# A hybrid decoder layer: group norms beside the latents, roots spread later, FFN matmul runs of 9, 9, 6

## The chip, the cores and the metric

The kernel runs on one core of one Trainium2 chip. The core has five engines that work side by side, each in the order of its own queue: TensorE (PE, with its weight loads as PEld), VectorE (DVE), ScalarE (ACT), GpSimd (POOL) and SyncE (SP, which issues transfers). They wait for each other by semaphores. The time is the device time of one execution in microseconds (us); what is compared is the median of several runs.

## The reference, cut to what matters

One layer with 256 tokens and a width of 2048, in float32. RMS norm, one input projection, two groups of heads side by side (16 RWKV-7 heads of 64 and 8 latent-attention heads), one output projection, residual; then RMS norm, a gated MLP of width 5632 with a causal convolution of width 3 on its gate, residual, and a final RMS norm.

```
h = rms_norm(x, attn_norm_g)
proj = h @ w_in
h_r, h_k, h_v, h_w, h_a, h_g = split(token_shift(proj[..., :RWKV_SHIFT_DIM], mu))
c_q, c_kv, k_pe = split(proj[..., RWKV_SHIFT_DIM:])          # 512, 512, 64 columns

# RWKV-7 group: a recurrence over the tokens, then a norm over each head
y = rwkv7_scan(r, decay, k, v, -kk, kk * a)
y = ((y - mean(y)) * rsqrt(var(y) + GN_EPS)) * gn_w + gn_b   # group norm
y_rwkv = (y + sum(r * k * r_k) * v) * (sigmoid(h_g) @ g2)

# latent attention group
q  = rms_norm(c_q, q_norm_g) @ w_uq
kv = rms_norm(c_kv, kv_norm_g) @ w_ukv
y_mla = softmax(causal(q @ k.T * scale)) @ v

x = x + concat(y_rwkv, y_mla) @ w_out
h = rms_norm(x, ffn_norm_g)
x = x + (silu(conv(h @ w_gate)) * (h @ w_up)) @ w_down
return rms_norm(x, final_norm_g)
```

## The kernel before

**Products.** Each float32 operand is split into a high part (hi, rounded to a matmul type) and the rest (lo), and a product is the sum of hi by hi, hi by lo and lo by hi. Weights come in pieces of 128x1024: `piece` lets SP load one, ACT cast it to hi and DVE subtract to get lo. `prod_c` multiplies a piece with 256 tokens at a time, `prod_a` with tokens on the output's partitions, and `prod_b`, used for the gate and up weights of the MLP, with moving blocks of 512 columns (256 of the activation's hi, 256 of its lo): 8 wide matmuls for the weight's hi, then 8 of 256 columns for its lo. `joined` and `scaled` take sums out of PSUM.

**Order.** The kernel's code emits operations; a scheduler simulates them and lays each engine's queue out by the place of emission as priority and by the buffers that it has (three PSUM buffers for sums called mm, three called ch, two called at). In the compiled program each engine's order is fixed. `tc.issue_after(x)` keeps an operation behind x, and `pend`/`flush` hand small jobs to the next tile.

**Stages.** (1) Input projection, tile by tile (`in_tile`), with the key, receptance and value tiles prepared for the recurrence. An opening part computes the decay: `wa` goes through a tanh on ACT and is multiplied by `lora`. (2) The recurrence: four chunks of 64 tokens (`chunk(c)`), serial, each with many small matmuls and copies between PE, DVE and ACT. The scheduler places tiles of the latents' projection between them. (3) `latent(0)` and `latent(1)`: four input tiles each for the query and the key-value latent, scaled out of PSUM into `cr`, split into `cl`, their squares summed in `css`; a sum over partitions (`pss`, copied to `ssm`), a root on POOL (`rsqrt`), the root `rr`, and by `bcast` (two matmuls with the diagonals `dg`, into `rsb`) its copy in all rows, `rrB`. (4) Up-projections: `up_b` for queries (`wuq`) and keys (`wuk`), `prod_a` for values (`wuv`). (5) `group_norm(w)` for each half w of the tokens: bonus values `bv`, means `gmu`, variances `gva` from squares `gsq`, a root of 16 columns on DVE, the norm's weights `gnw`, `gnb`, the gate `pgate` (two matmuls on `g2a`, `g2b`), then four transposes (`pyT`) and the split into `yhi`, `ylo` for the output projection. It is emitted behind all up-projections, interleaved with the attention heads (`heads`, with `scores` and `attend`). (6) Output projection, (7) MLP in two blocks of 24 and 20 tiles of 128 columns, (8) down-projection and final norm.

Of the kernel before, what the change touches and what calls it, by code (L numbers as in the profile page):

```python
# [54 lines left out]
def hybrid_layer(ctx: ExitStack, tc: tile.TileContext, a: dict, out: bass.AP):  # L55
# [109 lines left out]
    def prod_b(acc, pieces, act, kt0, n, first, last):  # L165
        hi, lo = pieces
        for j in range(n):
            PE.matmul(acc, hi[:, j * P:(j + 1) * P], act(kt0 + j), start=first and j == 0, stop=False,  # L168
                      skip_group_check=True)
        for j in range(n):  # L170
            PE.matmul(acc[:, :T], lo[:, j * P:(j + 1) * P], act(kt0 + j)[:, 0, :], start=False,  # L171
                      stop=last and j == n - 1, skip_group_check=True)

    def prod_c(acc, pieces, act, kt0, n, first, last):
        hi, lo = pieces
        for j in range(n):
            for s in range(2):
                PE.matmul(acc[:, :T], hi[:, j * P:(j + 1) * P], act(kt0 + j)[:, s, :],  # L178
                          start=first and j == 0 and s == 0, stop=False)
        for j in range(n):  # L180
            PE.matmul(acc[:, :T], lo[:, j * P:(j + 1) * P], act(kt0 + j)[:, 0, :], start=False,  # L181
                      stop=last and j == n - 1)
# [10 lines left out]
    def prod_a(accs, pieces, act_hi, act_lo, kt0, n, first, last, tbs=(0, 1)):  # L193
        hi, lo = pieces
        for j in range(n):
            wh, wl = hi[:, j * 512:(j + 1) * 512], lo[:, j * 512:(j + 1) * 512]
            for tb in tbs:
# [4 lines left out]
                PE.matmul(accs[tb], al, wh, start=False, stop=last and j == n - 1)  # L202
# [124 lines left out]
    S.activation(warm, ones[:, 0:2], AF.Sin)  # L327
# [78 lines left out]
    S.activation(wa[0:64], wa[0:64], AF.Tanh)
# [390 lines left out]
    def latent(x, gname, post):  # L797
# [22 lines left out]
        rb = con([P, T], f"rrB{x}")  # L820
        bcast(rr, rb, at, t2)
# [1 line left out]
        rrB.append(rb)
# [3 lines left out]
    latent(1, "kvg", 1.0)
    flush(True)
# [7 lines left out]

    def up_b(src, i, x, dsts):
        pcs = piece(src[i])
        for j in range(2):
            acc = mm()  # L840
            prod_c(acc, (pcs[0][:, j * 512:(j + 1) * 512], pcs[1][:, j * 512:(j + 1) * 512]),
                   lambda k: cl[x][k // 2][:, k % 2, :, :], 0, 4, True, True)
            scaled(dsts[j], acc, rrB[x])
# [8 lines left out]
    g2a = s4(n="g2a")  # L852
    g2b = s4(n="g2b")
    gnwb = [s4(n=n) for n in ("gnw", "gnb")]
    with tc.issue_after(ylast[1]):
        for t, n in zip(gnwb, ("gnw", "gnb")):
            nc.scalar.dma_start(t, a[n].broadcast_to([P, 1024]))
        nc.scalar.dma_start(g2a, a["g2"][0:P])
# [134 lines left out]
    for blk, nf in enumerate((24, 20)):  # L993
        hh = [s4(F32R, "hh").rearrange("p (k t) -> p k t", k=4) for _ in range(nf // 4)]
        hl = [s4(F32R, "hl").rearrange("p (k t) -> p k t", k=4) for _ in range(nf // 4)]
        for fi in range(nf):
# [1 line left out]
            accs = []
            for gu in range(2):
                acc = mm()  # L1000
                for h in range(2):
                    prod_b(acc, piece(a["wgu"][f, gu, h]), z_hl, h * 8, 8, h == 0, h == 1)
                accs.append(acc)
# [126 lines left out]
```

## Time and profile before

| | |
|---|---|
| median of 3 runs | 1191.4 us (1191.02 to 1200.56) |
| profiled execution | 1189.71 us |
| its span | 1187.9 us |
| mean granted TensorE clock | 0.993 |
| PE busy | 1161.1 us (98%), 7673 matmuls |
| DVE busy | 807.2 us (68%) |
| ACT busy | 590.5 us (50%) |
| POOL busy | 32.7 us (3%) |
| read from HBM | 210.58 MB, 180 GB/s over the span |

The span is the time between the first and the last record of the profiled execution. Rows of the timeline begin with the start in us from the span's beginning and the duration in us; then come the engine, the line, the operation, output and inputs, the shapes and the number of operations that the row groups. Brackets give idle time of that engine ahead of the row and what ended it.

### The profile page before, as it was taken

Reading aid. Unit: us, or ns where it says so; the run is one execution under the profiler, and the core shown is the slowest. Engines: PE = TensorE matmul, PEld = TensorE weight load, DVE = VectorE, ACT = ScalarE, POOL = GpSimd, SP = SyncE. Lnnn points to the kernel's source line nnn. Section 1 sums busy time; section 2 is a strip of 40 time slices with the busy share of each in tenths; the row PEclk is TensorE's granted clock in tenths of the full one; section 3 lists DMA queues with packets and bytes.
Section 4 is the critical chain, followed back from the end, with each engine's and each line's share of the span. In section 5 each row is a group of like instructions: output and inputs, shape, how many; then the busy total and the mean of one; then the engine's idle time right before and its main releaser. Section 6 shows DMA issues by size and latency. Waiting matters only on the chain.

```text
span 1187.9 us, 19414 instructions
## 1 busy us (share of the span) xinstructions
PE 1161.1 (98%) x7673; PEld 1022.6 (86%) x7673; DVE 807.2 (68%) x1301; ACT 590.5 (50%) x895; POOL 32.7 (3%) x87
## 2 busy tenths in 40 slices
PE   8999999998979999999999999999999999999996
PEld 8899999987958888888888888888888888888885
DVE  5898669745976567777777775444577777775663
ACT  6794345433425456555555554333455555544541
POOL 1200000003000001000000000000000000000000
PEclk9999999998999999999999999999999999999998
DMA  8635455714425555555555555665555555566662
GB/s 312 219 113 178 134 171 194 228 43 152 155 89 178 165 188 178 196 194 188 187 193 194 189 188 192 192 197 189 201 189 191 189 195 194 186 226 210 198 217 82
DMA packets 71035, 215.98 MB, mean 182 GB/s; under 512 B 17616, under 2 KB 17872, under 8 KB 70944
## 3 DMA queue, kind: packets, MB, share of 16 engines
q1 hardware_dynamic: 69776, 211.84, 54.3%
q10 hardware_dynamic: 768, 2.05, 0.5%
q0 software_dynamic: 400, 0.85, 0.3%
q8 instruction: 60, 0.98, 0.3%
q14 instruction: 31, 0.25, 0.1%
HBM read 210.58 MB, written 3.41 MB: 180 GB/s over the span
## 4 chain that ended last, share of the span: by engine, by line
PE 90%; DVE 4%; DMA 2%; POOL 1%; ACT 1%; issue 1%; SPq 0%; ACTq 0%; DVEq 0%; POOLq 0%
PE mm L168 27%; PE mm L171 14%; PE mm L178 10%; PE mm L200 9%; PE mm L201 9%; PE mm L202 9%; PE mm L181 5%; PE pg L545 1%; DVE lo L139 1%; PE px L694 1%; PE py L694 1%; DMA xraw<-in_xT 1%; DMA xt<-in_x 1%; DVE bv L752 0%; DMA raw<-in_win 0%
## 5 line engine op out<-in xcount | busy, mean ns | idle before, releaser
L139 DVE TENSOR_TENSOR lo<-raw,hi 128x1024 fp32r<-128x1024 f32 x376 | 459.9, 1223 | 278.7 <-ACT hi L138 273.5
L138 ACT CAST hi<-raw 128x1024 fp32r<-128x1024 f32 x376 | 395.0, 1051 | 471.8 <-PE mm L202 126.3
L168 PE MATMUL mm<-z,hi 128*128 128x512 f32 x1408 | 351.2, 392 | 0.0
L168 PEld LDWEIGHTS mm<-z,hi 128*128 128x128 f32 x1408 | 251.9, 188 | 43.7
L171 PEld LDWEIGHTS mm<-z,lo 128*128 128x128 f32 x1408 | 188.2, 188 | 14.5
L171 PE MATMUL mm<-z,lo 128*128 128x256 f32 x1408 | 191.5, 278 | 0.0
L178 PE MATMUL mm<-x,hi 128*128 128x256 f32 x1024 | 137.9, 283 | 2.1 <-ACT x L148 1.4
L178 PEld LDWEIGHTS mm<-x,hi 128*128 128x128 f32 x1024 | 126.0, 190 | 5.8 <-issue 1.7
L201 PE MATMUL mm<-lo,hh 128*128 128x512 f32 x336 | 130.7, 389 | 0.0
L202 PE MATMUL mm<-hi,hl 128*128 128x512 f32 x336 | 130.7, 389 | 0.0
L200 PE MATMUL mm<-hi,hh 128*128 128x512 f32 x336 | 119.7, 389 | 0.0
L202 PEld LDWEIGHTS mm<-hi,hl 128*128 128x128 f32 x336 | 63.1, 188 | 13.1
L200 PEld LDWEIGHTS mm<-hi,hh 128*128 128x128 f32 x336 | 63.1, 188 | 13.1
L201 PEld LDWEIGHTS mm<-lo,hh 128*128 128x128 f32 x336 | 63.1, 188 | 13.0
L181 PE MATMUL mm<-x,lo 128*128 128x256 f32 x512 | 73.7, 281 | 0.1
L181 PEld LDWEIGHTS mm<-x,lo 128*128 128x128 f32 x512 | 65.0, 188 | 1.1 <-issue 0.7
L201 PE MATMUL mm<-lo,yhi 128*128 128x512 f32 x128 | 51.1, 399 | 0.0
L202 PE MATMUL mm<-hi,ylo 128*128 128x512 f32 x128 | 50.3, 394 | 0.0
L200 PE MATMUL mm<-hi,yhi 128*128 128x512 f32 x128 | 49.5, 402 | 0.5 <-ACT yhi L788 0.3
L200 PEld LDWEIGHTS mm<-hi,yhi 128*128 128x128 f32 x128 | 24.0, 188 | 7.4 <-issue 1.5
L202 PEld LDWEIGHTS mm<-hi,ylo 128*128 128x128 f32 x128 | 24.1, 188 | 5.6 <-DVE bv L752 0.8
L201 PEld LDWEIGHTS mm<-lo,yhi 128*128 128x128 f32 x128 | 24.1, 188 | 4.5
(281 smaller groups left out, 1051.8 us busy)
## 6 DMA issues: line engine op xcount, KB each, us to landing
raw<-in_wgu SPq DMA_DIRECT2D x176, 512.0 KB, 4.2
raw<-in_wdn SPq DMA_DIRECT2D x88, 512.0 KB, 4.1
raw<-in_win SPq DMA_DIRECT2D x70, 512.0 KB, 3.7
raw<-in_wout SPq DMA_DIRECT2D x32, 512.0 KB, 3.4
raw<-in_wuq SPq DMA_DIRECT2D x6, 512.0 KB, 4.7
xraw<-in_xT SPq DMA_DIRECT2D x4, 512.0 KB, 8.4
xt<-in_x SPq DMA_DIRECT2D x4, 512.0 KB, 6.8
raw<-in_wuv SPq DMA_DIRECT2D x4, 512.0 KB, 3.4
```

The costliest lines, as they stand in the source:

```text
L138: S.copy(hi, raw)
L139: last_lo[0] = V.tensor_tensor(lo, raw, hi.bitcast(F32), ALU.subtract).ins
L168: PE.matmul(acc, hi[:, j * P:(j + 1) * P], act(kt0 + j), start=first and j == 0, stop=False, skip_group_check=True)
L171: PE.matmul(acc[:, :T], lo[:, j * P:(j + 1) * P], act(kt0 + j)[:, 0, :], start=False, stop=last and j == n - 1, skip_group_check=True)
L178: PE.matmul(acc[:, :T], hi[:, j * P:(j + 1) * P], act(kt0 + j)[:, s, :], start=first and j == 0 and s == 0, stop=False)
L181: PE.matmul(acc[:, :T], lo[:, j * P:(j + 1) * P], act(kt0 + j)[:, 0, :], start=False, stop=last and j == n - 1)
L200: PE.matmul(accs[tb], ah, wh, start=first and j == 0, stop=False)
L201: PE.matmul(accs[tb], ah, wl, start=False, stop=False)
L202: PE.matmul(accs[tb], al, wh, start=False, stop=last and j == n - 1)
L545: PE.matmul(pg[h][:, o:o + P], BK[pp][hs, gg, w * 2 + r, :, :], AR[pp][hs, gg, w * 2 + r, :, :], start=o == 0, stop=True, skip_group_check ...
L694: ins.append(PE.matmul(dst[HS[h], a_ * 64:(a_ + 1) * 64], lhsT, rhs, start=begin and n == 0 and a_ == 0, stop=True, skip_group_check=True) ...
```

## The change

Four things. The warm-up activation of ACT is a tanh in the place of a sine, and the tile `wa` is emitted with high priority. `group_norm(0)` is emitted between the two latents and `group_norm(1)` behind the second, and with them go the loads of their tables and the buffers that they use. The spreading of the two roots over the rows (`bcast` into `rrB`) leaves `latent`, and is emitted behind the first products of the queries and of the values, which are now both done before they are scaled. In the MLP's first half the hi matmuls of several pieces are emitted as runs of 10, 8, then 9, 9, 6 repeated, with the eight lo matmuls of one piece behind each run.

```
-    def prod_b(acc, pieces, act, kt0, n, first, last):
-        hi, lo = pieces
-        for j in range(n):
-            PE.matmul(acc, hi[...], act(kt0 + j), start=first and j == 0, stop=False, ...)
-        for j in range(n):
-            PE.matmul(acc[:, :T], lo[...], act(kt0 + j)[:, 0, :], start=False, stop=last and j == n - 1, ...)
+    def prod_b(n, src, act, done):
+        pcs, accs, g = {}, {}, 0
+        for q, run in enumerate(runs_of(2 * n)):
+            for _ in range(run):
+                p, j = divmod(g, 8)
+                i, h = divmod(p, 2)
+                if j == 0:
+                    pcs[p] = piece(src(i, h))
+                    if h == 0:
+                        accs[i] = mm()
+                PE.matmul(accs[i], pcs[p][0][:, j * P:(j + 1) * P], act(h * 8 + j), start=h == 0 and j == 0, ...)
+                g += 1
+            i, h = divmod(q, 2)
+            lo = pcs.pop(q)[1]
+            for j in range(8):
+                PE.matmul(accs[i][:, :T], lo[:, j * P:(j + 1) * P], act(h * 8 + j)[:, 0, :], start=False, ...)
+            if h == 1:
+                done(i, accs.pop(i))
+
+    def runs_of(n):
+        full, tail = (10, 8) + (9, 9, 6) * 7 + (6,), (10, 8, 9, 6, 9, 9, 6, 7)
+        return full * (n // 24) + tail * (n % 24 // 8)
...
-    S.activation(warm, ones[:, 0:2], AF.Sin)
+    S.activation(warm, ones[:, 0:2], AF.Tanh)
...
-    wa = shifted(acc0[0], 0, dst=early[:, 2 * T:3 * T])
-    S.activation(wa[0:64], wa[0:64], AF.Tanh)
+    with tc.high_priority():
+        wa = shifted(acc0[0], 0, dst=early[:, 2 * T:3 * T])
+        S.activation(wa[0:64], wa[0:64], AF.Tanh)
...
         V.tensor_scalar(rr, rsqrt(m, 1.0 / 512, EPS, 2), post, None, ALU.mult)
-        rb = con([P, T], f"rrB{x}")
-        bcast(rr, rb, at, t2)
...
     latent(0, "qg", SC)
+    g2a = s4(n="g2a")
+    g2b = s4(n="g2b")
+    gnwb = [s4(n=n) for n in ("gnw", "gnb")]
...
+    yhi = [[s4(F32R, "yhi").rearrange("p (k t) -> p k t", k=4) for _ in range(2)]]
+    ylo = [[s4(F32R, "ylo").rearrange("p (k t) -> p k t", k=4) for _ in range(2)]]
+    group_norm(0)
     latent(1, "kvg", 1.0)
+    group_norm(1)
     flush(True)
...
+    def spread(x, behind):
+        with tc.issue_after(behind):
+            bcast(rrs[x], rrB[x], at, t2)
...
+            end = prod_c(acc, (pcs[0][:, j * 512:(j + 1) * 512], pcs[1][:, j * 512:(j + 1) * 512]),
...
+        if src is a["wuq"] and i == 4:
+            spread(0, end)
+        for j in range(2):
+            scaled(dsts[j], accs[j], rrB[x])
...
         for tb in range(2):
             S.activation(vm[tb][:, cc * 512:(cc + 1) * 512], accs[tb], AF.Copy, scale=rrs[1][:, tb:tb + 1])
+        if cc == 0:
+            spread(1, end)
...
-    group_norm(0)
-    heads(0, 1)
-    group_norm(1)
-    heads(2, 3)
+    heads(0, 1, 2, 3)
```

What this does to the engines' queues. First PE behind the last chunk of the recurrence (py is a chunk's output; mm_3644 is the last input tile of `latent(1)`, with x_65 to x_68 its inputs). Before, the sum of squares is followed by the spread of the root and a whole input tile:

```order
L694 MATMUL py_3042<-UV_1878,G_1756 64x64 x8
L815 MATMUL pss_3406<-ones,css_3135 128x2 x2
L242 MATMUL rsb_3431<-dg_3432,ones 128x128
L242 MATMUL rsb_3431<-dg_3435,ones 128x128
L178 MATMUL mm_3644<-x_65,hi_3647 128x256 x8
L178 MATMUL mm_3644<-x_66,hi_3647 128x256 x8
L181 MATMUL mm_3644<-x_65,lo_3648 128x256 x4
L181 MATMUL mm_3644<-x_66,lo_3648 128x256 x4
L178 MATMUL mm_3644<-x_67,hi_3677 128x256 x8
L178 MATMUL mm_3644<-x_68,hi_3677 128x256 x8
L181 MATMUL mm_3644<-x_67,lo_3678 128x256 x4
L181 MATMUL mm_3644<-x_68,lo_3678 128x256 x4
```

After, an up-product of the queries (mm_3869), the transposes and gates of `group_norm(0)` and the next up-product stand there; the input tile, now mm_3706, lies between the chunks further ahead.

```order
L836 MATMUL pss_3406<-ones,css_3135 128x2 x2
L196 MATMUL mm_3869<-cl_3133,hi_3865 128x256 x4
L196 MATMUL mm_3869<-cl_3134,hi_3865 128x256 x4
L199 MATMUL mm_3869<-cl_3133,lo_3866 128x256 x2
L199 MATMUL mm_3869<-cl_3134,lo_3866 128x256 x2
L806 MATMUL pyT_3480<-cst,yt_2725 128x128 x4
L801 MATMUL pgate_3490<-g2a_3431,sg_611 128x512
L802 MATMUL pgate_3490<-g2b_3432,sg_612 128x512
L806 MATMUL pyT_3494<-cst,yt_2725 128x128 x4
L801 MATMUL pgate_3832<-g2a_3431,sg_611 128x512
L802 MATMUL pgate_3832<-g2b_3432,sg_612 128x512
L196 MATMUL mm_3882<-cl_3133,hi_3865 128x256 x4
```

The spread of the root has moved behind, and the transposes, which need the finished group norm, have come between two products.

DVE at the same place (cr takes an input tile out of PSUM). Before, the copy ssm of the sum of squares is followed by the root's spread and the latent's tiles:

```order
L817 COPY ssm_3409<-pss_3406 128x2
L819 TENSOR_SCALAR rr_3411<-ry_3413 128x2
L241 TENSOR_SCALAR dg_3432<-cst,rr_3411 128x128
L241 TENSOR_SCALAR dg_3435<-cst,rr_3411 128x128
L190 TENSOR_TENSOR cr_3503<-mm_3442,rsB 128x256
L812 SCALAR_TENSOR_TENSOR cl_3439<-cr_3503,vec,cl_3439 128x256
L243 COPY rrB_3430<-rsb_3431 128x256
L190 TENSOR_TENSOR cr_3569<-mm_3508,rsB 128x256
L809 TENSOR_TENSOR css_3441<-css_3441,csq_3571 128x256
L812 SCALAR_TENSOR_TENSOR cl_3439<-cr_3569,vec,cl_3439 128x256
L190 TENSOR_TENSOR cr_3637<-mm_3576,rsB 128x256
```

After, the group norm's rows on yt_2725 begin right behind it, with the root's row rr_3411 between two of its reductions:

```order
L838 COPY ssm_3409<-pss_3406 128x2
L209 TENSOR_TENSOR cr_3631<-mm_3570,rsB 128x256
L788 TENSOR_REDUCE gmu_3447<-yt_2725 128x8 x2
L789 TENSOR_SCALAR gmu_3447<-gmu_3447 128x16
L791 TENSOR_TENSOR yt_2725<-yt_2725,gmu_3447 128x512 x2
L794 TENSOR_REDUCE gva_3448<-gsq_3449 128x8
L840 TENSOR_SCALAR rr_3411<-ry_3413 128x2
L794 TENSOR_REDUCE gva_3448<-gsq_3449 128x8
```

Then, behind the eleven operations of the group norm's root and six of its products, its last rows and the first ones of the latent:

```order
L803 TENSOR_TENSOR yt_2725<-yt_2725,pgate_3476 128x512
L810 TENSOR_TENSOR ylo_3441<-pyT_3480,yhi_3439 128x4x128
L803 TENSOR_TENSOR yt_2725<-yt_2725,pgate_3490 128x512
L810 TENSOR_TENSOR ylo_3442<-pyT_3494,yhi_3440 128x4x128
L833 SCALAR_TENSOR_TENSOR cl_3501<-cr_3565,vec,cl_3501 128x256
L833 SCALAR_TENSOR_TENSOR cl_3501<-cr_3631,vec,cl_3501 128x256
L830 TENSOR_TENSOR css_3503<-css_3503,csq_3633 128x256
L209 TENSOR_TENSOR cr_3699<-mm_3638,rsB 128x256
```

The copies cr of the latent's tiles three and four (cr_3699 is the third) have moved behind the group norm.

ACT between two chunks (the copies to yt_2725 are the output of chunk(1); XB_2730<-px_2926 and UV_1877 belong to chunk(2)). Before:

```order
L744 COPY yt_2725<-py_2813 64x4x64 x2
L744 COPY yt_2725<-py_2814 64x4x64 x2
L720 COPY XB_2730<-px_2926 128x256
L728 COPY UV_1877<-px_2925 64x4x64
L728 COPY UV_1877<-px_2926 64x4x64
```

After, three of the four loads of the group norm's tables are issued between the last output copy of chunk(1), which is ylast[1], and the copy that chunk(2) needs:

```order
L765 COPY yt_2725<-py_2813 64x4x64 x2
L765 COPY yt_2725<-py_2814 64x4x64 x2
L851 DMA gnw_3433<-in_gnw 128x1024
L851 DMA gnb_3434<-in_gnb 128x1024
L852 DMA g2a_3431<-in_g 128x1024
L741 COPY XB_2730<-px_2926 128x256
L853 DMA g2b_3432<-in_g 32x1024
```

The loads have moved here from behind the query products, and chunk(2)'s copy stands behind them.

Last PE in the MLP (z the activations, mm the sums). Before, each piece's hi matmuls are followed by its lo matmuls:

```order
L168 MATMUL mm_5634<-z_4837,hi_5637 128x512 x4
L168 MATMUL mm_5634<-z_4838,hi_5637 128x512 x4
L171 MATMUL mm_5634<-z_4837,lo_5638 128x256 x4
L171 MATMUL mm_5634<-z_4838,lo_5638 128x256 x4
L168 MATMUL mm_5634<-z_4839,hi_5659 128x512 x4
L168 MATMUL mm_5634<-z_4840,hi_5659 128x512 x4
L171 MATMUL mm_5634<-z_4839,lo_5660 128x256 x4
L171 MATMUL mm_5634<-z_4840,lo_5660 128x256 x4
```

After, the hi matmuls run ahead of the lo ones of the piece, here the end of a run of 9, a run of 6 and another of 6:

```order
L177 MATMUL mm_9882<-z_4837,hi_9878 128x512 x4
L183 MATMUL mm_9822<-z_4839,lo_9857 128x256 x4
L183 MATMUL mm_9822<-z_4840,lo_9857 128x256 x4
L177 MATMUL mm_9882<-z_4838,hi_9878 128x512 x4
L177 MATMUL mm_9882<-z_4839,hi_9901 128x512 x2
L183 MATMUL mm_9882<-z_4837,lo_9879 128x256 x4
L183 MATMUL mm_9882<-z_4838,lo_9879 128x256 x4
L177 MATMUL mm_9882<-z_4839,hi_9901 128x512 x2
L177 MATMUL mm_9882<-z_4840,hi_9901 128x512 x4
L183 MATMUL mm_9882<-z_4839,lo_9902 128x256 x4
L183 MATMUL mm_9882<-z_4840,lo_9902 128x256 x4
```

The runs no longer end where a piece ends.

More of the change, by code (lines that the diff above doesn't have):

```diff
@@ L161, in flush @@
             f()
[L165 to L172 removed]
+    def prod_b(n, src, act, done):
[8 more added lines that the diff above has]
+                        accs[i] = mm()
+                PE.matmul(accs[i], pcs[p][0][:, j * P:(j + 1) * P], act(h * 8 + j), start=h == 0 and j == 0,
+                          stop=False, skip_group_check=True)
+                g += 1
+            i, h = divmod(q, 2)
+            lo = pcs.pop(q)[1]
+            for j in range(8):
+                PE.matmul(accs[i][:, :T], lo[:, j * P:(j + 1) * P], act(h * 8 + j)[:, 0, :], start=False,
+                          stop=h == 1 and j == 7, skip_group_check=True)
+            if h == 1:
[3 more added lines that the diff above has]
+        return full * (n // 24) + tail * (n % 24 // 8)
     def prod_c(acc, pieces, act, kt0, n, first, last):
@@ L180, in prod_c @@
         for j in range(n):
-            PE.matmul(acc[:, :T], lo[:, j * P:(j + 1) * P], act(kt0 + j)[:, 0, :], start=False,
-                      stop=last and j == n - 1)
+            i = PE.matmul(acc[:, :T], lo[:, j * P:(j + 1) * P], act(kt0 + j)[:, 0, :], start=False,
+                          stop=last and j == n - 1)
+        return i.ins
     def joined(dst, acc, scale):
@@ L201, in prod_a @@
                 PE.matmul(accs[tb], ah, wl, start=False, stop=False)
-                PE.matmul(accs[tb], al, wh, start=False, stop=last and j == n - 1)
+                i = PE.matmul(accs[tb], al, wh, start=False, stop=last and j == n - 1)
+        return i.ins
     x_hl = lambda k: xs_[k // 4][:, k % 4, :, :]
@@ L819, in latent @@
         V.tensor_scalar(rr, rsqrt(m, 1.0 / 512, EPS, 2), post, None, ALU.mult)
[L820 to L821 removed]
         rrs.append(rr)
[L823 removed]
+        rrB.append(con([P, T], f"rrB{x}"))
         cl.append(c_)
     latent(0, "qg", SC)
[L827 to L851 removed]
     g2a = s4(n="g2a")
@@ L995, in hybrid_layer, with ffn_tile @@
         hl = [s4(F32R, "hl").rearrange("p (k t) -> p k t", k=4) for _ in range(nf // 4)]
-        for fi in range(nf):
+        gates = {}
+        def ffn_tile(i, acc):
+            fi = i // 2
             f = f0 + fi
[L998 to L1003, printed above, removed]
+            if i % 2 == 0:
+                gates[fi] = acc
+                return
             gt = hbuf()
-            joined(gt[:, 2:258], accs[0], rs2B)
+            joined(gt[:, 2:258], gates.pop(fi), rs2B)
             cv = t1("cv")
```

44 lines of the change are left out of this document (27 added, 17 removed).

## Prediction

> **What bounds the kernel now.** I read the page first, then the windows of 30 us, then PE's waits, then the timeline around the longest of them.
>
> ```profile
> PE 1161.1 (98%) x7673; PEld 1022.6 (86%) x7673; DVE 807.2 (68%) x1301; ACT 590.5 (50%) x895; POOL 32.7 (3%) x87
> ```
> This is busy time, with its share of the span. PE is the bound, and only about 27 us of the span of 1187.9 are not PE. A change gains by filling PE's holes or by shortening matmuls, and loses by making holes.
>
> ```profile
> 240.00:270.00 30.00, 27.81 (x741) 25.25 (x741) 11.24 (x25) 12.45 (x31) 0.77 (x4) 1.00 0.12 38
> 270.00:300.00 30.00, 26.52 (x156) 23.26 (x157) 20.27 (x37) 11.42 (x17) 10.53 (x28) 0.89 0.55 180
> 330.00:360.00 30.00, 23.71 (x97) 15.40 (x96) 21.76 (x47) 8.70 (x20) 0.00 (x0) 0.94 0.24 76
> ```
> Columns: window, length, busy PE, PEld, DVE, ACT, POOL, granted clock, DMA share, GB/s. The holes lie in the middle of the program, between the recurrence's chunks (240 to 268) and the output projection. In the second and third rows the granted clock falls too: a long hole is paid twice.
>
> ```profile
> PE rsb L242 <- DVE dg L241: 4.8, 1, 4.8
> PE psc L879 <- ACT pexp L891: 4.3, 1, 4.3
> PE pyT L785 <- DVE yt L782: 1.5, 1, 1.5
> ```
> These are PE's longest waits (total, times, longest). The first is the latent's root behind the chunks; the other two are the attention heads and the second group norm.
>
> **The chunks: +8.4.** In the order after the change the last tile of the kv latent (48 matmuls into mm_3706) and one pgate pair stand between the chunks' matmuls; before, that tile was PE's filler behind them.
>
> ```profile
> 278.55 1.98 PE L178 MATMUL mm<-x,hi 128*128 128x256 f32 x16
> 280.37 1.07 PE L181 MATMUL mm<-x,lo 128*128 128x256 f32 x8
> ```
> Start to start, 16 matmuls took 1.82 us, or 114 ns each, so 48 are 5.5 us. I add 1.5 us for six more switches between these and the chunks' small matmuls (an estimate: the lone one before took about 0.2 to 0.3 us more than its share), 0.95 for the pgate pair, and take off 1.5 for chunk waits that are filled. The tables' loads come into the chunks as well:
>
> ```profile
> 257.32 0.74 ACT L744 COPY yt<-py 64x256 f32<-64x256 f32 x2 [0.49 <-PE py L694]
> 258.08 0.37 ACT L720 COPY XB<-px 128x256 f32<-128x256 f32 x1
> ```
> ```profile
> 282.04 0.33 ACTq L857 DMA_DIRECT2D gnw<-in_gnw  x1
> ...
> 282.89 0.74 ACTq L858 DMA_DIRECT2D g2a<-in_g  x1
> ```
> ```profile
> gnb<-in_gnb ACTq DMA_DIRECT2D x1, 512.0 KB, 6.8
> g2a<-in_g ACTq DMA_DIRECT2D x1, 512.0 KB, 9.3
> ```
> The issues now stand directly behind ylast[1] (the copy at 257.32) and ahead of chunk 2's XB copy (258.08): gnw, gnb and g2a hold ACT from 282.04 to 283.63, so XB comes 1.5 us later, and the chunk with it. Then DVE's bv + gnb, which waits for gnb's landing, stands ahead of the four state updates of chunk 2, and the pgate pair waits for g2a in chunk 3. By the landings of before (6.8 and 9.3 us, with two weight pieces in flight beside them) both would be late by up to 5 us; in this stretch DMA is 0.12 busy, so they should land sooner. I take 0.5 us, bounds 0 to 5. Sum: 5.5 + 1.5 + 0.95 − 1.5 + 1.5 + 0.5 = 8.45, and the chunks' end E moves from 268.1 to about 276.5.
>
> **From E to the value projection: +13.6, the largest term.**
>
> ```profile
> 268.08 0.61 PE L815 MATMUL pss<-ones,css 128*128 128x2 f32 x4 [0.30 <-ACT yt L744]
> 268.72 0.16 DVE L817 COPY ssm<-pss 128x2 f32<-128x2 f32 x1 [2.07 <-PE pss L815]
> ...
> 272.85 0.17 DVE L819 TENSOR_SCALAR rr<-ry 128x2 f32<-128x2 f32 x1 [3.97 <-POOL ry L233]
> ...
> 273.49 1.20 PE L242 MATMUL rsb<-dg,ones 128*128 128x128 f32 x4 [4.80 <-DVE dg L241]
> ...
> 287.45 0.40 PE L200 MATMUL mm<-hi,cl 128*128 128x512 f32 x1
> ```
> Before, PE waited 4.8 us here for the root and reached the value projection (L200) 19.4 us behind E. After, the root's spread is out of PE's way, but PE has just pss and one up-product of 12 matmuls (1.4 us) ahead of pyT_3480, the first transpose of the group norm. That one waits for DVE's yt*pgate, so the whole of group_norm(0) runs exposed. It is a serial chain, and DVE's queue holds it ahead of cr_3699, which frees the PSUM buffer of the next up-product. Its links:
>
> ```profile
> 335.36 0.17 DVE L228 TENSOR_TENSOR rt<-rt,rm 128x16 f32<-128x16 f32 x1
> 335.56 0.18 DVE L230 SCALAR_TENSOR_TENSOR ry<-rt,ry 128x16 f32<-128x16 f32 x1
> ```
> ```profile
> 337.61 1.29 DVE L777 TENSOR_TENSOR yt<-yt,gnw 128x512 f32<-128x512 f32 x2
> ```
> ```profile
> 288.85 1.22 DVE L139 TENSOR_TENSOR lo<-raw,hi 128x1024 fp32r<-128x1024 f32 x1
> ...
> 288.95 1.17 POOL L227 TENSOR_TENSOR rt<-ry 128x2 f32<-128x2 f32 x1
> ```
> ssm ends at E+0.8, cr at E+1.2, two gmu reductions (128x512 each, as in the row at 337.61: 1.2 us the pair) and their scaling at E+2.6, the subtraction pair at E+3.8. Behind the first half of gva DVE's queue holds rr, which waits for POOL: 4.1 us from ssm by the rows at 268.72 and 272.85, plus some 1.2 because a POOL step of 0.2 us took 1.17 us beside a DVE operation with two wide inputs (288.95); so E+6.0. The second half of gva (0.6) and eleven dependent small operations at 0.2 us give E+8.9, three pairs at 1.2 us (yt with ry, gnw, bv) E+12.6, the gate's product 0.7: **pyT starts at about E+13.4**, and PE has stood idle some 11 us and runs at half clock when it resumes. Then yhi and ylo of two halves, two cl and css bring cr_3699 to E+21.
>
> ```profile
> 296.88 2.44 DVE L752 TENSOR_TENSOR bv<-UV,bon 64x1024 f32<-64x1024 f32 x2
> ```
> Behind it DVE has the second group's bv (2.4 us) and bv + gnb (1.2) ahead of cr_3767 (E+26), then css, dg, gmu and the qr copies, on which the third and fourth up-products wait (E+26 and E+31). The value projection starts at about E+33, or 309.5, against 287.45: **22.05 us later**, of which 8.4 are E's.
>
> The Trainium skill says in "SBUF — State Buffer" (section "SBUF: two separate sides") that DVE and GpSimd take their shared port pair as an exclusive lock for the whole instruction; the 1.17 us at 288.95 agree, and by that rule the root may come later still, by a DVE operation (1.2 us) per POOL step that meets one. It says in "TensorE: Matmul & The Clock Gate" (section "HAM oscillation — how this bites in real kernels") that idle gaps of PE over about 3.4 us drop its clock, which speaks against a change that puts 11 us in the place of 4.8; the 0.89 in the second window agrees.
>
> **Given back later: −10.85.** The second group norm is mostly done by 309, and the heads find DVE free. The waits of 4.3 and 1.5 us, two small ones of 0.5 together, and 1.7 us at half clock behind 335 should go: 8.0. Three pgate pairs (0.95 each) and two sets of transposes (0.5 each) are already done: 3.85. I put 1.0 on the other side for new small stalls among the heads; the cover that hides the rest is the up-projections' PE work.
>
> **FFN runs: −2.0.**
>
> ```profile
> 501.90 1.07 PE L171 MATMUL mm<-z,lo 128*128 128x256 f32 x8
> 502.80 1.99 PE L168 MATMUL mm<-z,hi 128*128 128x512 f32 x8
> 504.63 1.11 PE L171 MATMUL mm<-z,lo 128*128 128x256 f32 x8
> ```
> ```profile
> 454.94 2.32 PE L168 MATMUL mm<-z,hi 128*128 128x512 f32 x9
> 457.10 1.07 PE L171 MATMUL mm<-z,lo 128*128 128x256 f32 x8
> ...
> 463.63 1.39 PE L168 MATMUL mm<-z,hi 128*128 128x512 f32 x5
> 464.86 1.11 PE L171 MATMUL mm<-z,lo 128*128 128x256 f32 x8
> ```
> With runs of 8 wide hi matmuls, every second run of lo matmuls is slow: 1.11 against 1.07, about 36 ns a run. Behind a run of 9 it was fast, behind 5 slow: the wide matmuls seem to cycle in three, and a lo run entered at a full cycle is fast. 88 of 176 are slow now; runs of 9, 9, 6 keep the full cycle, and only the 10, 8, 9 that open a block of 24 pieces leave it, which by my count makes 27 slow: 61 × 0.036 = 2.2, taken as 2.0. Bounds −3.2 (all fast) to +3.2 (all slow). PE never waits in this phase, and pieces still come one at a time.
>
> **Opening: −1.0.**
>
> ```profile
> 48.94 0.91 PE L426 MATMUL lw<-early,lora 64*128 64x256 f32 x3 [0.99 <-ACT early L406]
> ```
> One activation table load of 1.28 us goes on ACT just ahead of this wait; the rest of the order is unchanged there, so the priority does nothing.
>
> **Sum.** 8.4 + 13.65 − 8.0 − 3.85 + 1.0 − 2.0 − 1.0 = +8.2. The profiled execution took 1189.7 with a span of 1187.9; the median of the runs is 1191.4, 1.7 more. So 1197.9 for a profiled execution, 1199.6 as a median; I say 1199.5.
>
> **Rivals.**
> 1. The group norm runs as DVE work without waits, and the fillers in the chunks are free. DVE's rows from E to the value projection sum to 23.3 us, so its start cannot come before about E+25; break-even of the whole change is near E+25 with E at 276.5. With E at 275 and the start at E+27 to E+30 (7.5 to 4.5 less than in the sum) the change costs 0.7 to 3.7, and with all lo runs fast 1.2 less: 1191 to 1195. For it: DVE is only 0.68 busy. Against: the links depend on each other, and the POOL root, ACT's squares and PE's transposes lie between them.
> 2. **Slower than before by over 1%**, the other side: the tables land late. gnb is issued some 0.7 us and g2a 1.5 us behind ylast[1]; at 6.8 and 9.3 us the chunks lose 4 to 5 us instead of 0.5, and the POOL root or the half clock add 1 to 3. Median 1204 to 1208. It decides from a landing of gnb of over 4 us. For it: those rows. Against: nearly empty queues there.
> 3. The FFN part does nothing, because a matmul costs the same in any run: +2.0, 1201.5; or the phase is met wrongly: +5. Against it stand the rows of 9 and 5. The Trainium skill, "TensorE: Matmul & The Clock Gate" (section "Wait — 56ns, not 53.3ns?"), gives N ÷ 2.4 GHz + 2.5 ns for each warm matmul, 215.7 ns at N = 512, whatever the run; here 8 took 1.83 us (502.80 to 504.63), 229 ns each, so the trace does not agree.
> 4. The scheduler's placement is not kept: excluded, since each engine runs its own queue in order.
>
> **How the numbers follow.** Forecast as worked (1195 to 1203): 0.55. Rival 1: 0.16. Rival 2: 0.20. Rival 3: 0.09, half of it inside 1203. The range takes 1191 to 1207, with E+28 and late tables inside it. A measurement of this kernel tells about 1% (11.9 us) from no change: faster by more would need a start of the value projection at E+13, which DVE's sum excludes save for an error of mine, 0.03; over 1203.3 come rival 2 and the forecast's tail, 0.25; within, 0.72.
>
> **What would show it.** Right: PE's longest wait is pyT on DVE's yt, 10 to 12 us, just behind the chunks, with a granted clock below 0.9 there; the first value projection matmul near 309; waits of psc and pyT near 335 and 351 gone; most lo runs at 1.07; no table load at 47. Wrong: PE's wait behind the chunks under 7 us (rival 1), a wait of px or pgate on a DMA in the chunks (rival 2), or 1.11 in half the lo rows (rival 3). An unseen wait among the heads would upset the −8.0.

## The result, and the profile after

The changed kernel takes 1201.03 us (median of 8, 1200.24 to 1203.0) against 1191.21 us for the kernel before on the same chip: a ratio of 1.0069, with a 95% interval of 1.0052 to 1.0087. It is slower by less than the 1% named above, and inside the forecast range of 1191 to 1207. The forecast was 1199.5. The profiled execution took 1200.9 us with a span of 1199.1.

The first line is busy time, as above; then the windows of the middle (columns as above):

```profile
PE 1162.9 (97%) x7673; PEld 1022.0 (85%) x7673; DVE 808.7 (67%) x1301; ACT 603.9 (50%) x894; POOL 29.6 (2%) x87
```
```profile
240.00:270.00 30.00, 28.73 (x595) 26.02 (x587) 12.63 (x21) 9.89 (x21) 0.00 (x0) 0.94 0.31 98
270.00:300.00 30.00, 16.76 (x196) 10.48 (x196) 18.12 (x44) 7.67 (x18) 3.65 (x14) 0.83 0.06 19
300.00:330.00 30.00, 22.64 (x112) 19.37 (x113) 24.46 (x50) 10.53 (x16) 5.58 (x18) 0.89 0.25 72
330.00:360.00 30.00, 29.64 (x223) 27.43 (x222) 23.90 (x43) 12.70 (x21) 0.00 (x0) 1.00 0.58 192
```
The holes have moved. The window from 330, which had 23.71 us of PE work, is full; the one from 270 has fallen to 16.76, at a granted clock of 0.83. PE's waits say why (total, times, longest):

```profile
PE pyT L806 <- DVE yt L803: 11.0, 2, 10.2
PE mm L196 <- DVE cr L209: 4.7, 3, 3.0
PE mm L220 <- DVE lo L139: 2.1, 1, 2.1
PE mm L196 <- DVE qr L209: 2.0, 1, 2.0
PE pgate L801 <- DMA g2a<-in_g: 1.6, 1, 1.6
```
The waits of rsb (4.8), psc (4.3) and the old pyT (1.5) are gone. In their place PE waits 10.2 us for the exposed norm, and then for the copies that DVE queues behind it. PE's timeline from the last gate pair in the chunks to the value projection:

```profile
270.32 1.10 PE L801 MATMUL pgate<-g2a,sg 128*128 128x512 f32 x2 [1.59 <-DMA g2a<-in_g]
271.35 1.12 PE L802 MATMUL pgate<-g2b,sg 32*128 32x512 f32 x2
272.40 1.15 PE L715 MATMUL py<-UV,G 128*64 128x64 f32 x32
...
278.46 0.61 PE L836 MATMUL pss<-ones,css 128*128 128x2 f32 x4 [0.30 <-ACT yt L765]
...
291.55 1.11 PE L806 MATMUL pyT<-cst,yt 128*128 128x128 f32 x4 [10.22 <-DVE yt L803]
...
300.21 1.22 PE L196 MATMUL mm<-cl,hi 128*128 128x256 f32 x8 [1.12 <-DVE cr L209]
...
304.89 1.82 PE L196 MATMUL mm<-cl,hi 128*128 128x256 f32 x8 [2.98 <-DVE cr L209]
...
311.06 1.30 PE L196 MATMUL mm<-cl,hi 128*128 128x256 f32 x8 [2.03 <-DVE qr L209]
...
313.00 0.63 PE L219 MATMUL mm<-hi,cl 128*128 128x512 f32 x1
```
With E at 278.46, pyT starts at E+13.1, the second to fourth up-products at E+21.8, E+26.4 and E+32.6, and the value projection at E+34.5; at 313.00 its matmuls still run at a lower clock (0.63 us against 0.39 at full clock).

The first starts of six stages in the two profiled executions give the ledger. The last two columns are what a stage added or gave back, and the prediction's term:

| first matmul of | before | after | later by | added | predicted |
|---|---|---|---|---|---|
| decay (lw) | 48.94 | 47.40 | −1.54 | −1.54 | −1.0 |
| chunks (px) | 241.19 | 240.32 | −0.88 | +0.66 | 0 |
| pss (E) | 268.08 | 278.46 | +10.38 | +11.26 | +8.4 |
| value projection | 287.45 | 313.00 | +25.56 | +15.18 | +13.65 |
| MLP, block 1 | 451.80 | 465.22 | +13.42 | −12.14 | −10.85 |
| last matmul | 1177.72 | 1188.90 | +11.18 | −2.23 | −2.0 |

The last row holds the MLP (−1.27 in its first block, −1.06 in its second) and 0.1 of the rest.

### The profile page after: what moved, and what is told of

The parts are those of the page before. It is cut to its first block, busy times and chain, and to the rows that moved or that the text cites. A ratio compares the mean times of both kernels' runs of the same rounds, so it can differ in the third digit from the quotient of the medians.

```text
span 1199.1 us, 19497 instructions
## 1 busy us (share of the span) xinstructions
PE 1162.9 (97%) x7673; PEld 1022.0 (85%) x7673; DVE 808.7 (67%) x1301; ACT 603.9 (50%) x894; POOL 29.6 (2%) x87
## 4 chain that ended last, share of the span: by engine, by line
PE 89%; DVE 3%; DMA 3%; ACT 2%; issue 1%; POOL 1%; SPq 0%; ACTq 0%; DVEq 0%
PE mm L177 27%; PE mm L183 13%; PE mm L196 10%; PE mm L219 9%; PE mm L221 9%; PE mm L220 9%; PE mm L199 5%; PE pg L566 1%; PE px L715 1%; DMA xraw<-in_xT 1%; PE py L715 1%; DVE lo L139 1%; DMA xt<-in_x 1%; DMA g2a<-in_g 1%; ACT hi L138 0%
## 5 line engine op out<-in xcount | busy, mean ns | idle before, releaser
L221 PEld LDWEIGHTS mm<-hi,hl 128*128 128x128 f32 x336 | 63.1, 188 | 13.1
L196 PE MATMUL mm<-cl,hi 128*128 128x256 f32 x160 | 24.4, 295 | 7.1 <-DVE cr L209 4.7
L196 PEld LDWEIGHTS mm<-cl,hi 128*128 128x128 f32 x160 | 21.1, 195 | 9.6 <-DVE cr L209 5.8
```

The source lines that it names most:

```text
L221: i = PE.matmul(accs[tb], al, wh, start=False, stop=last and j == n - 1)
```

## Experiments

Ratios are to the kernel before in the same runs, with 95% intervals. Stages are read from the same marks as in the ledger.

**One part alone: the opening** (e1_open), on the kernel before.

```
-    S.activation(warm, ones[:, 0:2], AF.Sin)
+    S.activation(warm, ones[:, 0:2], AF.Tanh)
...
+    with tc.high_priority():
         wa = shifted(acc0[0], 0, dst=early[:, 2 * T:3 * T])
```

> The kernel before with the opening's part alone (the warm-up activation a tanh, the tile wa at high priority). Theory: the wait of 0.99 us at 48.94 goes with the table load ahead of it, and nothing later takes it back but the drift that the full change shows up to the chunks; 0.9 us faster, between 0.5 and 1.5, with one table load fewer. Rival: the load only hides behind something else, and the time is the same within 0.3 us.

1191.5 us, ratio 0.9997 (0.9982 to 1.0012). The first lw stands at 47.40 as in the full change, 1.54 earlier, and 0.8 of it is left at the chunks; but the chunks then took 28.4 us (240.40 to 268.76) in the place of 26.9:

```profile
240.00:270.00 30.00, 28.69 (x715) 25.98 (x709) 11.30 (x25) 11.92 (x31) 0.26 (x2) 0.94 0.10 33
```
The queues are the same there, but the clock is 0.94 in the place of 1.00. Four executions with these chunks at full clock (before, e2_runs, e6_best, e7_mid) took 26.9 us for them, so one stretch of 3.4 us at half clock cost 1.5. So a us gained at 49 can be lost at 240 to the clock; the runs cannot tell the opening from nothing.

**One part alone: the MLP runs** (e2_runs), on the kernel before.

```
-                    prod_b(acc, piece(a["wgu"][f, gu, h]), z_hl, h * 8, 8, h == 0, h == 1)
...
+        prod_b(2 * nf, lambda i, h: a["wgu"][f0 + i // 2, i % 2, h], z_hl, ffn_tile)
```

> The kernel before with the runs of 10, 8, 9, 9, 6 in the MLP alone. Theory (a run of narrow lo matmuls costs 0.906 us when the wide ones before it ended a cycle of three, and 0.944 otherwise): some 25 slow runs of 176 in the place of 89, 64 x 0.037 = 2.3 us faster, all of it between the first wide matmul and the last narrow one. Rival (a matmul costs the same in any run, and the 2.3 us in the full change come from something earlier, such as pieces that arrive sooner): the same within 0.5 us.

1189.72 us, ratio 0.9977 (0.9957 to 0.9997), 2.4 us less. Up to the MLP's first matmul this execution is 2.15 us later than the one of before, at the last one 0.17 earlier: 2.32 in the MLP, as in the full change. Read run by run, from a lo run's first matmul to the next hi matmul, 150 of the 175 whole lo runs of after took 0.91 us and 25 took 0.94; before it was 87 and 89. In the steady part of after:

```profile
485.93 1.07 PE L183 MATMUL mm<-z,lo 128*128 128x256 f32 x8
486.84 1.53 PE L177 MATMUL mm<-z,hi 128*128 128x512 f32 x6
488.21 1.07 PE L183 MATMUL mm<-z,lo 128*128 128x256 f32 x8
489.12 2.22 PE L177 MATMUL mm<-z,hi 128*128 128x512 f32 x9
491.18 1.07 PE L183 MATMUL mm<-z,lo 128*128 128x256 f32 x8
```
Every lo run here, behind 6 or 9, takes 0.91 us from start to start. Of the 25 that take 0.94, 20 stand behind the 10, 8 and 9 that open a block of 24, four in the broken runs at the MLP's start and one behind the last run of 7. The cycle of three can be read from the single records: wide matmuls last 388, 392 and 394 ns in turn, and all 405 fast lo runs of before, after and e6_best follow one of 394 ns, while 121 of the 122 slow ones follow another. Nothing else moves in this stretch: from its first matmul to the program's last the six profiled kernels with runs of 8 (before and e1, e3, e4, e10, e12) took 725.92 us each, those with 10, 8, 9, 9, 6 mostly 723.6 to 723.7 (724.7 in e9_cut_after).

**The norms and the spreads without the rest** (e3_norms), on the kernel before.

```
     latent(0, "qg", SC)
+    group_norm(0)
     latent(1, "kvg", 1.0)
+    group_norm(1)
...
+            spread(0, end)
...
+            spread(1, end)
```

> The kernel before with the group norms beside the latents and the spreads later, without the opening's part and without the MLP runs. Theory (the norms are the whole loss): by the two traces' marks 11.3 us lost up to the chunks' end, 15.2 from there to the value projection, 12.1 given back up to the MLP: 12 to 14.5 us slower, some 1204 to 1205, with PE's wait of pyT on yt at about 10 us. Rival (the parts hamper each other, for instance the chunk stretch is slow because the opening has shifted it): less than 9 us slower.

1204.91 us, ratio 1.0111 (1.0085 to 1.0138), with a wait of 10.2 us of pyT on yt. The theory's 12 to 14.5 us came (12.8 by the medians): the whole loss is here, and the other parts hide 3 us of it by the medians, 5 by the ratios, whose intervals touch. The profiled execution, 1211.74 us, is the longest of the six, with PE at half clock for 23.9 us from 292 on, so its middle stages are not compared here.

**The spreads alone** (e4_spread), on the kernel before; the calls of `group_norm` stay where they were.

```
-        bcast(rr, rb, at, t2)
...
+            spread(0, end)
...
+            spread(1, end)
```

> The kernel before with the spreads of the two roots alone emitted behind the first products; the group norms stay behind the up-projections. In its order too the last latent tile moves into the chunks, and an up-product. Theory (the loss in the full change is the exposed group norm chain, and the moved spread is good): PE's wait of 4.8 us for the root and the half clock behind it go, the chunks' end comes 7 to 9 us later with one tile and one product more in them, the value projection starts 4 to 7 us earlier: 4 to 6 us faster, about 1186. Rival (the work moved into the chunks costs more there than it saves behind them): the same within 2 us or slower, with the value projection at 287 or later.

1196.35 us, ratio 1.0033 (1.0018 to 1.0048): 4 us slower, so the theory fell. In its profile the chunks take 37.2 us in the place of 26.9 (241.78 to 278.94); 7.7 us come back between E and the value projection (11.7 in the place of 19.4), and 3.1 are lost up to the MLP, where PE's wait of pyT is 4.0 in the place of 1.5. The chunk stretch has little room:

```profile
240.00:270.00 30.00, 29.84 (x589) 27.01 (x591) 11.17 (x23) 11.47 (x24) 0.00 (x0) 0.89 0.18 56
```
Before, PE was busy 27.81 of the 30 us there. A tile of 5.5 us and a product of 1.4 put into that stretch cost about their own length, and here a lower clock (0.89) came on top: 6.8 us at half clock from 240, some 3 us by the price of e1_open.

**The norms alone** (e12_norms_only), on the kernel before, with `bcast` left in `latent`.

```
     latent(0, "qg", SC)
+    group_norm(0)
     latent(1, "kvg", 1.0)
+    group_norm(1)
```

> The kernel before with the group norms alone emitted beside the latents; the roots' spreads stay in the latents, and the opening and the MLP runs are those of before. In its order the last latent tile and one product stay behind the chunks, ahead of the norm's transposes. Theory (the two moves make the loss together: the later spread sends the tile into the chunks, and without it PE has nothing to do while the norm runs): PE's wait of pyT is under 3 us, the chunks' end comes some 4 us later (gate pair and tables) and not 10, the value projection some 12 us later, 12 us are given back later: within 3 us of before, and well under 1200. Rival (the two moves add up): the norms cost what e3_norms has over e4_spread, 8 to 9 us: 1199.5 to 1201, with a wait of pyT of 6 us or more.

1204.83 us, ratio 1.0126 (1.0107 to 1.0145). The cover worked, but the theory of a joint loss fell, and with it the rival, whose 1199.5 to 1201 and wait of 6 us did not come either:

```profile
PE rsb L242 <- DVE dg L241: 10.6, 2, 6.1
PE pgate L780 <- DMA g2a<-in_g: 3.4, 1, 3.4
...
PE pyT L785 <- DVE yt L782: 0.8, 1, 0.8
```
pyT waits 0.8 us behind the last tile, but the root's spread now stands behind the norm's first rows on DVE and waits 6.1 us, the second root's 4.5, and the tables 3.4. With the spread in its old place the norm costs 14.6 us by the medians, with the later spread 12.8 (e3_norms; the intervals overlap), although the later spread alone costs 4. The parts do not add: whatever PE needs from DVE behind the chunks waits for the norm that DVE has queued ahead of it.

The chunks themselves were the larger miss. They took 37.3 us (242.13 to 279.38), 10.4 more than before and not 4, although the latent's tile is not among them:

```profile
266.72 2.05 PE L780 MATMUL pgate<-g2a,sg 128*128 128x512 f32 x2 [3.39 <-DMA g2a<-in_g]
268.70 2.07 PE L781 MATMUL pgate<-g2b,sg 32*128 32x512 f32 x2
```
PE waits 3.4 us for the table, the gate pair behind it takes 4.0 us at half clock, and the half clock lasts until 276.1. The spreads alone added 10.3 us to the chunks, the norms alone 10.4, both together 11.3: the tile that the later spread sends into the chunks fills about half of PE's wait for the tables (1.6 us are left of 3.4).

**The tables one chunk earlier** (e5_tables), on the changed kernel.

```
-    with tc.issue_after(ylast[1]):
+    with tc.issue_after(ylast[0]):
         for t, n in zip(gnwb, ("gnw", "gnb")):
```

> The changed kernel with the four table loads issued one chunk earlier (behind ylast[0] in the place of ylast[1]). Theory (late tables cost some 3 us of the chunk stretch): PE's wait of 1.6 us for g2a and DVE's of 3.6 us for gnb go, the state updates of chunk 2 come earlier, the chunks' end moves 2 to 4 us forward, and the time is 2 to 4 us under the changed kernel's. Rival (the issues only delay another chunk's copy, and PE's fillers hide the wait): less than 1 us.

1198.2 us, ratio 1.0053 (1.0033 to 1.0072), against 1201.03 and 1.0069: 2.8 us by the medians, 1.9 by the ratios, whose intervals overlap. PE's list of waits has no transfer left in it:

```profile
PE pyT L806 <- DVE yt L803: 11.5, 3, 10.2
PE mm L196 <- DVE cr L209: 5.6, 3, 3.9
PE pT L684 <- issue: 1.5, 1, 1.5
```
The time agrees with the theory, its mechanism is not shown: the chunks took 37.7 us in the profiled execution against 38.1 in the changed kernel's. Its clock there was 0.89 against 0.94, twice as long at half clock, which by the price of e1_open would hide some 1.5 us. The 1.2 us by which its last matmul comes earlier arise behind the value projection.

**PE kept busy while it would wait** (e8_warm). On the changed kernel, in `group_norm`:

```
             pt = ch("pyT")
+            if w == 0 and j == 0:
+                with tc.issue_after(pss_end[0]):
+                    for _ in range(9):
+                        PE.matmul(pt, ones, g2a[:, 0:512], start=True, stop=True)
```

> The changed kernel with nine matmuls on ones and g2a put behind the first pss, into the PSUM buffer of the first pyT, whose result is overwritten; the output is unchanged. They keep PE busy while it would wait for the norm, and the second gate pair slides ahead of the transposes. Theory (the half clock and the gate at half clock behind the wait cost 3 to 5 us): the wait of 10 us shrinks to 2, the granted clock stays at 1.00 from 270 to 300, the value projection starts 3 to 6 us earlier and the time is 1195 to 1198. Rival (only the exposed chain costs): the value projection starts within 1.5 us of 313, the time is within 1.5 us of the changed kernel's.

1195.02 us, ratio 1.0020 (1.0005 to 1.0035): 6 us under the changed kernel.

```profile
270.00:300.00 30.00, 24.00 (x226) 14.29 (x224) 22.41 (x49) 9.53 (x21) 3.66 (x14) 1.00 0.05 19
300.00:330.00 30.00, 27.93 (x155) 25.32 (x156) 25.06 (x53) 11.85 (x15) 5.56 (x18) 0.83 0.40 126
```
```profile
290.69 1.25 PE L811 MATMUL pyT<-cst,yt 128*128 128x128 f32 x8 [1.13 <-DVE yt L804]
```
Work that computes nothing saves 6 us by the medians, and the two ratios' intervals lie apart. pyT still starts at E+13.1, so the chain is as long as before; but the clock stays at 1.00 up to 300, and the second gate pair, which slid ahead, no longer holds up the second half. The value projection starts at E+31.7 in the place of E+34.5. Which share of these 2.8 us is the clock's and which the gate's was not separated. Between the two profiles 3.5 us more are saved from there to the MLP, where the changed kernel ran at half clock from 312.0 to 315.4 and waited 2.1 us for lo, and 1.2 in the chunks, where the clock did not fall at 240; the fillers, which come later, can't have done the last. Nor do they end the half clock: it comes at 299.9, for 10.2 us, in the next gap of PE:

```profile
300.79 2.07 PE L197 MATMUL mm<-cl,hi 128*128 128x256 f32 x8 [4.11 <-DVE cr L210]
```

**Five steps of the norm left out,** in the changed kernel (e9_cut_after) and in the one before (e10_cut_before).

```
+        if w == 1:
+            for j in range(2):
+                V.tensor_reduce(mu[:, hs[j]], v3(y, j), AX.X, ALU.add)
+            V.tensor_scalar(mu, mu, 1.0 / 64, None, ALU.mult)
...
+            if w == 1:
+                V.tensor_tensor(v3(y, j), v3(y, j), wide(mu, j), ALU.subtract)
...
+            if w == 1:
+                V.tensor_tensor(y[:, cs[j]], y[:, cs[j]], gnwb[0][:, cs[j]], ALU.mult)
+                V.tensor_tensor(y[:, cs[j]], y[:, cs[j]], bv[:, cs[j]], ALU.add)
```

> The changed kernel with five DVE steps of group_norm(0) left out (the sum for the mean and its scaling, the subtraction of the mean, the products with gnw and the sum with bv; the output then lacks them for the first half of the tokens): some 5.0 us of DVE work. Theory (the chain behind the chunks is exposed, every us of it is a us of PE's wait): pyT starts 5 to 6 us earlier behind the chunks' end, and the time is 4.5 to 7 us under the changed kernel's. Rival (something else is the limit there: the root on POOL, ACT's squares, or the table loads): less than 3 us.

> The kernel before with the same five DVE steps of group_norm(0) left out (the output lacks them as well). Theory (there the norm runs beside the up-projections' matmuls): 0 to 1.5 us faster, the gain being what DVE's full stretch from 300 to 334 passes on to the heads. Rival (the norm was on the path there too): 3 us or more faster.

Changed kernel: 1197.67 us, ratio 1.0041 (1.0022 to 1.0060), 3.4 us under 1201.03, with overlapping intervals. Kernel before: 1189.18, ratio 0.9972 (0.9949 to 0.9994), 2.8 us less. By the medians both lie between theory and rival; the second interval, 0.7 to 6.1 us, leaves room for either. In the changed kernel pyT starts at E+7.5 in the place of E+13.1, as expected, but only 2.2 of these 5.6 us arrive at the value projection (E+32.3). PE ran at half clock from 278, when its up-product took 1.78 us, to 312, and each of its two gate pairs took 3.9 us there, where the changed kernel's took 3.3 and 2.1:

```profile
270.00:300.00 30.00, 22.23 (x206) 14.24 (x204) 15.75 (x35) 9.35 (x21) 2.81 (x14) 0.64 0.04 13
300.00:330.00 30.00, 26.93 (x126) 22.45 (x126) 25.05 (x52) 11.36 (x15) 5.56 (x18) 0.79 0.35 105
```
```profile
285.23 1.92 PE L804 MATMUL pgate<-g2a,sg 128*128 128x512 f32 x2
287.07 2.07 PE L805 MATMUL pgate<-g2b,sg 32*128 32x512 f32 x2
```
The 2.8 us before suggest that the norm was not free there either; how they reach the end was not settled, and the profiled executions (1189.45 and 1189.71 us) differ by 0.3 alone. Since the two gains can't be told apart, this pair does not show that a us of the norm is worth more where it is exposed. What it shows is that the norm sets the start of pyT.

**The norms elsewhere** (e7_mid), on the kernel of e6_best, which is told next.

```
+    group_norm(0)
     for i in range(4):
         up_b(a["wuq"], i, 0, [qn[:, i * 2 + j, :] for j in range(2)])
...
+    group_norm(1)
+    heads(0, 1, 2, 3)
```

> The kernel of e6_best with group_norm(0) emitted between the value projection and the query and key up-projections, and group_norm(1) behind those. Theory (a norm's chain is free where PE has products queued ahead of its transposes): PE's waits of 4.3 and 1.5 us among the heads shrink, no wait of pyT over 2 us comes, and the time is 3 to 8 us under e6_best's. Rival (DVE is full in that stretch, 29.7 of 30 us busy, so its copies of products and lo parts come later by what the norm takes): within 2 us of e6_best or slower, with PE waiting on DVE's lo, qn or kn.

1190.41 us, ratio 0.9986 (0.9971 to 1.0001), 2.9 us more than e6_best by the medians, with overlapping intervals: the theory's gain did not come. The time is the rival's, the waits that it named are not: of lo, qn and kn PE's list has 0.4 us for qn alone. The waits of psc shrink from 4.3 to 3.3 in two, and one of pyT grows to 3.4:

```profile
PE rsb L260 <- DVE dg L259: 4.8, 1, 4.8
PE pyT L804 <- DVE yt L801: 4.0, 2, 3.4
PE psc L898 <- ACT pexp L910: 3.3, 2, 1.9
```

**A version that beats both** (e6_best). The kernel before with the opening's part and with runs of 9, 9, 6 alone:

```
-        full, tail = (10, 8) + (9, 9, 6) * 7 + (6,), (10, 8, 9, 6, 9, 9, 6, 7)
+        full, tail = (9, 9, 6) * 8, (9, 9, 6, 9, 9, 6, 9, 7)
```

> The kernel before with the opening's part and with MLP runs of 9, 9, 6 throughout, no 10 and 8 at the start of a block of 24; group norms and spreads as before. Theory (cycle of three): no more than a few slow lo runs of 176, 3.2 us less than before in the MLP, 0 to 0.9 from the opening: 1187.5 to 1189. Rival (the 10 and 8 are needed since pieces come late without them, or the slow runs come from something else every 24 pieces): PE waits on hi or lo in the MLP, or 20 or more slow runs, and no more than 2.4 us gained.

1187.54 us, ratio 0.9962 (0.9944 to 0.9980). 8 of 176 lo runs take 0.94 us; the MLP takes 3.0 us less than before, and no wait on hi or lo comes up in it. Then, on this kernel, fillers ahead of the first root's spread (e11_warmroot):

```
     pb = pf("rsb")
+    if warm:
+        with tc.issue_after(pss_end[0]):
+            for _ in range(warm):
+                PE.matmul(pb[:, 0:384], ones, cst[:, 0:384], start=True, stop=True)
```

> The kernel of e6_best with six matmuls on ones and the constants (384 columns) put into the buffer of the first root's spread, behind the first pss, overwritten by the spread; the output is unchanged. They fill 4 of the 4.8 us in which PE waits for the root. Theory (the idle stretch costs its own length and then a half clock from 270.5 to 277): rsb starts where it did, the 16 matmuls behind it take 2.0 and not 3.5 us, and the time is 1.5 to 2.5 us under e6_best's. Rival (the clock falls for another reason, or the fillers delay the spread): within 0.7 us of e6_best, or slower.

1186.55 us, ratio 0.9948 (0.9931 to 0.9966). The two intervals overlap, so the step between them is shown by its stretch: from pss to the value projection 17.8 us (269.20 to 287.02) against 19.4 in e6_best and before, at full clock:

```profile
274.54 0.71 PE L265 MATMUL rsb<-dg,ones 128*128 128x128 f32 x4 [0.43 <-DVE dg L264]
275.07 2.15 PE L197 MATMUL mm<-x,hi 128*128 128x256 f32 x16
```
The 16 matmuls behind the root took 2.15 us, 1.55 us are saved in the stretch, and 1.0 by the medians: under the forecast of 1.5 to 2.5. This is the fastest version here, 0.5% under the kernel before and 1.2% under the changed one.

## Why the prediction was right, and where its terms were off

**The exposed norm.** This step carried the forecast, and it held: pyT at E+13.1 (13.4 forecast), the next three up-products at E+21.8, 26.4 and 32.6 (21, 26 and 31). DVE was busy 25.4 of the 34.5 us up to the value projection, near the 23.3 that rival 1 summed; the rest is the waits between the links, which rival 1 left out. The rows of before were enough for it because the order of DVE's queue, not a cost, decides what PE waits for. DVE's rows at the two ends of the chain, and the root between them:

```profile
279.10 0.16 DVE L838 COPY ssm<-pss 128x2 f32<-128x2 f32 x1 [2.07 <-PE pss L836]
...
284.11 0.17 DVE L840 TENSOR_SCALAR rr<-ry 128x2 f32<-128x2 f32 x1 [1.02 <-POOL ry L253]
...
290.82 0.68 DVE L803 TENSOR_TENSOR yt<-yt,pgate 128x512 f32<-128x512 f32 x1
```
The root came 5.0 us behind ssm, where the forecast had 4.1 + 1.2:

```profile
281.02 1.29 DVE L791 TENSOR_TENSOR yt<-yt,gmu 128x512 f32<-128x512 f32 x2
281.04 0.73 POOL L247 TENSOR_TENSOR rt<-ry 128x2 f32<-128x2 f32 x1
281.84 0.53 POOL L248 TENSOR_TENSOR rt<-rt,rm 128x2 f32<-128x2 f32 x1
```
Two POOL steps of 0.20 took 0.73 and 0.53 beside DVE's pair with two inputs. That fits the exclusive port lock of the Trainium skill's "SBUF — State Buffer" (section "SBUF: two separate sides"), with one blocked step per DVE operation and no more.

The term was 1.5 short (15.18 against 13.65) behind pyT, where the half clock was counted once and stayed, on and off, up to 315 (284.7 to 294.9, 305.2 to 308.6, 312.0 to 315.4).

**The chunks: mis-sized, 11.26 against 8.4.** Two of its terms were wrong. The gate pair was taken at 0.95 us; that was the pitch of one of its two matmuls. The pair took 2.08 (270.32 to 272.40). And a clock that fell at 240 (1.12 us for the first 16 matmuls of px, 0.69 before) cost 1.5 us by the price of e1_open, which had no term. It is not the change's: e1_open and e4_spread met it as well, e8_warm, with the changed kernel's chunks, did not. The landings, rival 2, came to 1.59 us of PE's wait against 0.5:

```profile
268.91 1.23 DVE L776 TENSOR_TENSOR bv<-bv,gnb 128x1024 f32<-128x1024 f32 x1 [3.64 <-DMA gnb<-in_gnb]
```
gnb landed 7.1 us and g2a 7.8 us behind their issues, as slowly as before although the other queues were nearly empty. What rival 2 said of the mechanism was right, and its sign, a wait of pgate on a transfer, came. Its price was smaller, because PE's tile filled part of the wait: in e12_norms_only, without the tile there, PE waits 3.4 us. The issues held ACT up less than the 1.5 us assumed:

```profile
262.36 0.33 ACTq L852 DMA_DIRECT2D g2a<-in_g  x1
262.79 0.37 ACT L741 COPY XB<-px 128x256 f32<-128x256 f32 x1 [0.72 <-PE px L715]
```
The copies ahead of XB ran beside the first two issues; the third ended at 262.69, 0.45 us behind the px that XB reads, so 0.5 us at most are the issues'. The rows of before had shown that an issue does not hold ACT's own work for its whole length, since this row lies within the 282.04 to 283.63 that the forecast counted as held:

```profile
282.31 0.49 ACT L811 ACTIVATE cl<-cr,vec 128x256 fp32r<-128x256 f32 x1
```
With these in the place of the forecast's, the terms come to 5.5 + 1.5 + 2.1 + 1.5 + 1.6 + 0.5 − 1.5 = 11.2. The tile, the switches and the filled waits (5.5, 1.5 and −1.5) were not measured one by one.

**Given back: 12.14 against 10.85.** The three gate pairs are worth 2.1 each and not 0.95, 3.4 more; new waits of 2.1 us for lo and 0.4 for qn, where 1.0 was put for all of them, take 1.5 of it away. That leaves 12.75, 0.6 more than came.

**MLP: right**, 2.33 against 2.0, and 25 lo runs of 0.94 us where 27 were counted. The Trainium skill's "TensorE: Matmul & The Clock Gate" (section "Wait — 56ns, not 53.3ns?") gives warm matmuls of 512 columns 215.7 ns from start to start, which does not hold for this mix. Here 9 wide ones took 2.06 us (489.12 to 491.18), 229 ns each, and the narrow run behind them depends on how many there were.

**Opening: not shown.** The wait at 49 went and the first lw stands 1.54 us earlier, but e1_open cannot tell its time from before. The eight profiled executions with this part reach the chunks at 240.7 on the mean and the six without it at 242.1, with overlapping ranges.

**The sum** was 8.2 us; the profiles differ by 11.2, the medians by 9.8, the ratio's interval says 6.2 to 10.4. The profiled execution of before was itself 1.5 us under its median. That the medians came within 1.6 us of the sum is in part luck: the stages missed by +2.9 (chunks), +1.5, −1.3 and smaller ones, 3.0 in all between the profiles, of which the medians show 1.6. The value projection, forecast near 309, came at 313.0.

## What to carry to other kernels

Before a chain is moved next to another stage, read what stands behind it in its engine's queue: the price is the sum of the chain's links up to the first thing that the busiest engine needs, and filling that engine elsewhere does not pay when the place it is filled from loses its cover. A change of several parts should be timed part by part: here the one part that gained (the MLP runs, 2.4 us) was hidden under one that lost 13. Where a wait can't be avoided, filling it with work that is thrown away can pay, since the wait is paid again in the clock.

## What the runs showed of the hardware

- A run of eight 256-column matmuls took 0.907 or 0.944 us, depending on where the 512-column ones ahead of it had stopped in a cycle of three (388, 392, 394 ns; fast behind the third). Runs of 9, 9, 6 in the place of 8 gained 3.0 us with the same matmuls (725.92 and 722.91 us from the MLP's start to the last matmul).
- PE's clock fell to half at about 240 in some executions and not in others of the same instructions (px of chunk 0: 1.12 or 0.69 us for 16 matmuls). Such a fall of 3.4 us cost 1.5 us in e1_open. The fourteen profiled executions also began the chunks anywhere between 239.9 and 243.8, so single profiles can differ by several us for reasons that are not the change's.
- Filling PE's idle stretch with nine useless matmuls took 6 us off the time by the medians (e8_warm), and shortening the chain by 5.6 us took off 3.4 (e9_cut_after, within the noise of the intervals). The rule of the Trainium skill's "TensorE: Matmul & The Clock Gate" (section "HAM oscillation — how this bites in real kernels"), that idle gaps of PE over some 3.4 us drop the clock, agrees with the first: without the gap of 10.2 us the clock stays at 1.00 up to 299.9, where it falls in a gap of 4.1 us. It does not explain the second, where the up-product ahead of the gap of 3.6 us was at half clock already.
